# Exchanging the resident operand of a seven-product matmul kernel: blocks in pairs in place of plain blocks

## The chip, the cores and the metric

The kernel runs on one core of a Trainium2 chip. The metric is the device time of one execution in microseconds, taken as the median of several runs. The inputs are fixed random arrays, all fp32.

## The reference

The reference is one layer of an encoder over 2048 tokens of 1024 channels: token mixing, cross-attention into 256 memory tokens, and a feed-forward network, each between two RMS norms and added to the residual stream.

```python
u = rms_norm(h, g_mix_pre); z = u @ w_in              # 1024 -> 2816
ya = swa_with_sinks(...)                              # window attention, 8 heads of 64
yh = hgrn2(...)                                       # gated recurrence, 4 heads of 128
y = concatenate([ya, yh]) @ w_out                     # 1024 -> 1024
h = h + rms_norm(y, g_mix_post)
u = rms_norm(h, g_x_pre); m = rms_norm(mem, g_mem)
y = cross_attention(u, m, wq, wk, wv, wo)             # 4 heads of 256
h = h + rms_norm(y, g_x_post)
u = rms_norm(h, g_ffn_pre)
y = (silu(u @ w_gate) * (u @ w_up)) @ w_down          # 1024 -> 2816 -> 1024
h = h + rms_norm(y, g_ffn_post)
```

## The kernel before

**Precision and products.** TensorE multiplies fp32r operands, so each fp32 operand is split into a rounded part and a rest (`split2`, line 871: ACT or POOL rounds, line 874 or 876, and DVE subtracts, line 877). A product of two such operands is three matmuls per tile of 128 rows (`products`, lines 1004 to 1006). On top of that the large matrix products use the Strassen-Winograd scheme: a block of 256 rows by 1024 columns is cut in two by two, and is made of seven half-size products (`seven`) where the plain way takes eight (`eight`). With four k tiles a product of half size is twelve matmuls, so a seven-product block has 84 and a plain one 96; with three k tiles it is 63 and 72.

**Operands.** Each product has a streamed side S and a resident side T. The S of a block come from two raw tiles (`streamed`, pool tag `raw`), from which DVE forms four sums (`combine`, line 979, tag `sum`) and `made` splits seven S tiles. The T tiles are 128 x 2 x 4 x 512 and serve all blocks of a job. There are seven slots for them. The seven T of a job are three quarters of the operand itself (keys 1, 2, 3) and four sums of quarters (keys 5, 7, 6, 4, `CHAIN`); a plain block needs the fourth quarter, key 8, and none of the sums.

**Jobs.** `jobs` lists what runs after the mixing stage: the output projection, the cross-attention scores with folded weights (`qk_d`), its values (`vo_d`), the feed-forward's first layer for two halves of the tokens (`ffn_u(b)`; here the tokens are the resident side and w_gate and w_up are streamed in turn), and three parts of the down projection (3, 4 and 4 pairs of k tiles). A job is a list of blocks of a kind: `"s"` is seven products, `"p"` is plain. The last block of every job but the last is plain, and so is the first block of the out projection and of the first feed-forward half (`kinds`, nine in all). In such a block the four sum slots are free, so the sums of the next job can be put in them.

**Sums made ahead.** For most jobs the four sums of T are made in an earlier stage and stored in DRAM (`sums` and `combined`, line 921): a tile half is then one load. For the out projection and the first feed-forward half (`None` in the job) they are made on the spot in `resident`: keys 5 and 7 take two loads per half and each sum a DVE operation of 128x1024 (line 903).

**Order.** `phases` writes the order out by hand. For each step it emits the product, then the S splits of the step after next (`upto(need[g + 2])`), then one turn of every generator in `after` (what follows a block: norms, transposes, stores), then the split of a T half that is due, and the loading of the next T half if a slot is free (`half`). T halves lie in row tiles (tag `row`, nine of them, used for results too) until they are split, two steps later. `behind` queues an instruction behind the last marked ones of ACT and DVE. When the program is built, a planner may put instructions of one engine in another order than the source has. In a seven-product block the steps are 1, 5, 6, 3, 7, 2, 4: products 1, 6, 7 and 4 accumulate in one PSUM bank, which ACT copies out after 1 and after 6 (line 1019), 5 and 3 in a second bank, 2 in a third. Six banks are for products and two for transposes.

**Ahead of the jobs** stand the input projection's first half (`in_first`, the same scheme), its second half beside the window attention and the recurrence (`in_proj`, `swa`, `hgrn`), and the folding of the cross-attention weights beside the rest of the recurrence (`fold_cross`). DMAs are issued from SP (lines 75 and 78), except those that add into a tile (line 1350), from POOL. Tokens pass from stage to stage as transposed tensors in DRAM: `y_d`, `h1t_d`, `pt_d`, `u_d`, each `[8, 128, 2048]`, so that a token tile of 128 is read and written in pieces of 512 B, and a block of 256 tokens in pieces of 1 KB.

Of the kernel before, what the change touches and what calls it, by code (L numbers as in the profile page):

```python
# [48 lines left out]
class Layer:  # L49
# [116 lines left out]
    def run(self):  # L166
# [4 lines left out]
        self.y_d = tc.dram_tile([KT, P, T], F32, name="y_d")  # L171
        self.un_d = tc.dram_tile([KT, P, TB], F32, name="un_d")
        self.h1t_d = tc.dram_tile([KT, P, T], F32, name="h1t_d")
        self.pt_d = tc.dram_tile([KT, P, T], F32, name="pt_d")
# [22 lines left out]
    def mix(self):  # L197
        tc, I = self.tc, self.I
        kw = dict(reuse_waits="tile")
        with contextlib.ExitStack() as left:  # L200
# [5 lines left out]
            with (  # L206
                tc.tile_pool(name="t1", bufs=3, **kw) as self.ts,
                tc.tile_pool(name="t2", bufs=3, **kw) as self.tb,
                tc.tile_pool(name="s1", bufs=2, side="right", **kw) as self.st_pool,
                contextlib.ExitStack() as at,  # L210
            ):
                self.banks(at, "ps1", **MOST)
                self.raws = 3
                u = self.in_first()
# [4 lines left out]
            with tc.tile_pool(name="sw", bufs=1, side="right", **kw) as self.sw:  # L219
# [16 lines left out]
            phases = self.phases(self.jobs(), None, lambda: self.io_tile("z"))  # L236
# [10 lines left out]
            with (  # L247
# [6 lines left out]
                self.raws = 4  # L254
# [151 lines left out]
    def in_first(self):  # L406
# [72 lines left out]
        blocks = [("q" if i == 0 else "p" if i < 2 else "s",)  # L479
# [34 lines left out]
    def in_block(self, ca, cb, beside, get, between):  # L514
# [19 lines left out]
        def out(i, j, a, b):  # L534
# [14 lines left out]
            else:  # L549
                self._n += 1  # L550
                t = self.st_pool.tile([P, 512], F32, tag="part", name=f"th_{self._n}", bufs=3)
# [163 lines left out]
    def swa_back(self, n, kinds, S, vs):  # L715
# [25 lines left out]
        self.store(self.y_d[0:4, :, n * P:(n + 1) * P].rearrange("k p t -> p k t"), ys)  # L741
# [84 lines left out]
    def hgrn_last(self, n, kinds, on, sg):  # L826
# [6 lines left out]
        self.store(self.y_d[4:8, :, n * P:(n + 1) * P].rearrange("k p t -> p k t"), sg)  # L833
# [33 lines left out]
    STEPS = {"s": (1, 5, 6, 3, 7, 2, 4), "p": (1, 2, 8, 3), "q": (1, 2, 8, 3)}  # L867
    TAKES = {"s": (1,) * 7, "p": (2, 2, 0, 0), "q": (4, 0, 0, 0)}
# [83 lines left out]
    def streamed(self, load, nk, kind, engine=None, tiled=False):  # L952
# [14 lines left out]
        yield None  # L967
# [8 lines left out]
        def combine(a, b, op):  # L976
            self._n += 1
            t = self.st_pool.tile([P, 4, P], F32, tag="sum", name=f"sum_{self._n}", bufs=3)[:, :nk, :]
# [7 lines left out]
        yield made(a11, "A")  # L986
        s1 = combine(a21, a22, ALU.add)
# [3 lines left out]
        yield made(combine(a12, s2, ALU.subtract), "A")  # L991
        yield made(combine(a11, a21, ALU.subtract), "P")
        yield made(a12, "A")
# [14 lines left out]
    def seven(self, S, T, nk, out, addend):  # L1008
# [6 lines left out]
        def copy(ps, i, j):  # L1015
            self._n += 1
            t = self.st_pool.tile([P, 512], F32, tag="part", name=f"part_{self._n}", bufs=3)
# [6 lines left out]
        for p in self.STEPS["s"]:  # L1024
# [60 lines left out]
    def phases(self, jobs, first, prologue=None):  # L1085

        steps = [(n, i, p) for n, job in enumerate(jobs) for i, b in enumerate(job[2])
                 for p in self.STEPS[b[0]]]  # L1090
        takes = [c for job in jobs for b in job[2] for c in self.TAKES[b[0]]]
        need = list(itertools.accumulate(takes)) + [sum(takes)] * 2
# [79 lines left out]
        blocks = [b for job in jobs for b in job[2]]  # L1172
        streams, ready, made = [], [], [0]

        def stream(at):
            if at < len(blocks):
                streams.append(blocks[at][1](blocks[at][0]))
                next(streams[-1])

        def upto(count):  # L1180
            while made[0] < count:
                s = next(streams[0], None)
                if s is None:
                    streams.pop(0)
                    continue
                ready.append(s)
# [9 lines left out]
        for i in range(2):  # L1196
            upto(need[i])
# [3 lines left out]
        at = 0  # L1201
        self.last = {}
        for _, nk, bl, _, beside in jobs:
            for i, (kind, _, out, follow, addend) in enumerate(bl):
                stream(at + 1)
                after += [f() for f in beside.get(i, ())]
                run = (self.seven(ready, Ready(), nk, out, addend) if kind == "s" else
                       self.eight(ready, Ready(), nk, out, addend, kind == "q"))
                for q in range(len(self.STEPS[kind])):
                    next(run)  # L1210
                    self.mark()
                    upto(need[g + 2])
                    for _ in range(1 if kind == "s" else 2):
# [10 lines left out]
                after.append(follow())  # L1224
                at += 1
# [20 lines left out]
    def jobs(self):  # L1246
# [24 lines left out]
        def sums(name, src, nk, other=None):  # L1271
            dst = self.tc.dram_tile([4, P, nk * 512], F32, name=name)

            def get(which, i, j, k0, n):
                t = (self.extra_tile, other or self.gain_tile)[which]().rearrange("p (k d) -> p k d", d=512)[:, :n]
# [10 lines left out]
        qk_s, vo_s = sums("qk_s", qk, 4, self.row_tile), sums("vo_s", vo, 4)  # L1286
        u_s = sums("u_s", ffn_u(1), 4)
        d_s = [sums(f"d_s{c}", src, nk) for c, (src, _, nk) in enumerate(down)]
        jobs = [(w_out, 4, kinds([self.mixed_block(n) for n in range(0, NT, 2)], 1), None, {2: [qk_s[1]]}),
                (qk, 4, kinds([self.score_block(n) for n in range(0, NT, 2)]), qk_s[0], {1: [vo_s[1]]}),  # L1290
                (vo, 4, kinds([self.value_block(n) for n in range(0, NT, 2)]), vo_s[0], {})]
        for b in range(NB):
            beside = {2: [in_turn(*(d[1] for d in d_s))]} if b else {4: [u_s[1]]}
            jobs.append((ffn_u(b), 4, kinds([blk for f in range(0, NFF, 2) for blk in self.hidden_blocks(b, f)], 1 - b),
                         u_s[0] if b else None, beside))
# [303 lines left out]
```

## Time and profile before

| what | value |
|---|---|
| median of 3 runs | 2636.8 us (2635.38 to 2640.75) |
| the profiled execution | 2634.33 us |
| its span in the trace | 2632.6 us |
| TensorE busy | 2555.3 us (97%), 12265 instructions |
| VectorE busy | 1712.0 us (65%) |
| ScalarE busy | 1261.0 us (48%) |
| granted TensorE clock, mean | 0.992 |

The span is what the trace covers; the execution's own time is 1.7 us longer. Busy shares are means over stages with different limits. In the trace of this kernel the lines 1004 to 1006 are the matmuls of the blocks, 877 and 874 the splits, 979 the sums of S, 1019 the copies of partial products, 1239 the transposes. The out projection's products run from about 795 us, the scores' from about 1000, the values' from about 1165, the feed-forward's from about 1345, the down projection's from about 2200 us.

### The profile page before, as it was taken

The numbers are of one execution on the slowest core, as the hardware profiler recorded it, in microseconds if no ns is written. First come the engines' busy times: TensorE is split into PE (matmuls) and PEld (weight loads), VectorE is DVE, ScalarE is ACT, GpSimd is POOL, SyncE is SP. The second block draws the span as 40 slices with busy tenths as digits, with TensorE's granted clock in tenths as the row PEclk, the third lists the DMA queues.
The fourth block names the chain that finished last, engine by engine and source line by source line (L and its number), as shares of the span: only waits on it lengthen the run. The fifth ranks groups of instructions, "written<-read, shape, count | busy, mean of one in ns | idle before, by whom it ended". The sixth has DMA issues, their size and how long they took to land.

```text
span 2632.6 us, 34672 instructions
## 1 busy us (share of the span) xinstructions
PE 2555.3 (97%) x12265; PEld 2129.9 (81%) x12265; DVE 1712.0 (65%) x2693; ACT 1261.0 (48%) x2620; POOL 465.6 (18%) x651
## 2 busy tenths in 40 slices
PE   7999999999999999999989999999999999999998
PEld 6877888887987777888878888888888888888886
DVE  7675578876556658777666655566666656574656
ACT  5463366655554556565564333344333334453543
POOL 4240344321412323323310000000000000000022
PEclk9999999999999999999999999999999999999999
DMA  5434655444887998776893632253556435576888
GB/s 184 145 130 167 201 153 164 131 155 151 254 292 207 285 284 256 213 243 176 227 285 129 192 111 80 98 192 127 168 198 202 153 117 176 179 216 179 266 209 215
DMA packets 331628, 494.46 MB, mean 188 GB/s; under 512 B 20416, under 2 KB 204736, under 8 KB 331456
## 3 DMA queue, kind: packets, MB, share of 16 engines
q1 hardware_dynamic: 320800, 453.46, 52.1%
q0 software_dynamic: 10656, 38.80, 8.2%
q8 instruction: 96, 1.57, 0.2%
q14 instruction: 76, 0.62, 0.1%
HBM read 333.85 MB, written 158.33 MB: 187 GB/s over the span
## 4 chain that ended last, share of the span: by engine, by line
PE 77%; DMA 11%; DVE 4%; ACT 3%; issue 3%; POOL 2%; SPq 0%; DVEq 0%; POOLq 0%; ACTq 0%
PE psm L1004 21%; PE psm L1005 21%; PE psm L1006 21%; PE psg L163 2%; PE psg L161 2%; PE psg L162 2%; PE pss L1239 1%; DMA z<-in_w_out_dram 1%; DMA h1t_d<-row 1%; DMA row<-in_w_out_dram 1%; DMA u_d<-row 1%; DMA row<-y_d 1%; DMA row<-in_x_dram 1%; DMA row<-u_d 1%; DMA sraw<-in_w_in_dram 1%
## 5 line engine op out<-in xcount | busy, mean ns | idle before, releaser
L1004 PE MATMUL psm<-T,S 128*128 128x512 f32 x2699 | 1049.3, 393 | 17.7 <-ACT part L1019 7.1
L1005 PE MATMUL psm<-T,S 128*128 128x512 f32 x2699 | 1054.6, 391 | 6.4 <-DVE T L877 6.4
L1006 PE MATMUL psm<-T,S 128*128 128x512 f32 x2699 | 1045.9, 391 | 2.1 <-DVE S L877 2.1
L1004 PEld LDWEIGHTS psm<-T,S 128*128 128x128 f32 x2699 | 509.3, 189 | 131.5 <-ACT part L1019 8.7
L1005 PEld LDWEIGHTS psm<-T,S 128*128 128x128 f32 x2699 | 509.2, 189 | 113.0 <-DVE T L877 8.6
L1006 PEld LDWEIGHTS psm<-T,S 128*128 128x128 f32 x2699 | 508.9, 189 | 109.8 <-DVE S L877 4.4
L877 DVE TENSOR_TENSOR S<-sraw,S 128x512 fp32r<-128x512 f32 (+1 forms) x320 | 222.9, 703 | 219.2 <-ACT S L874 199.7
L874 ACT ACTIVATE S<-sum 128x512 fp32r<-128x512 f32 (+1 forms) x310 | 186.1, 618 | 343.0 <-PE psm L1006 245.8
L877 DVE TENSOR_TENSOR S<-sum,S 128x512 fp32r<-128x512 f32 (+1 forms) x368 | 247.6, 683 | 58.4 <-ACT S L874 37.7
L1019 ACT ACTIVATE part<-psm 128x512 f32<-128x512 f32 x270 | 159.8, 596 | 244.1 <-PE psm L1006 225.2
L874 ACT ACTIVATE S<-sraw 128x512 fp32r<-128x512 f32 (+1 forms) x273 | 168.0, 617 | 122.4 <-PE psm L1006 103.5
L1350 POOL DMA_DIRECT2D row<-y_d x28 | 25.9, 926 | 1123.7 <-DVE row L1523 1038.3
L877 DVE TENSOR_TENSOR T<-row,T 128x1024 fp32r<-128x1024 f32 (+1 forms) x122 | 144.2, 1195 | 63.1 <-ACT T L874 62.7
L1321 ACT ACTIVATE junk<-row 128x512 f32<-128x512 f32 x160 | 99.9, 626 | 89.0 <-DVE row L1343 29.7
L161 PE MATMUL psg<-u,whi 128*128 128x512 f32 x352 | 141.1, 401 | 1.1 <-POOL whi L145 1.1
L163 PE MATMUL psg<-u,wlo 128*128 128x512 f32 x352 | 139.6, 397 | 1.5 <-DVE wlo L146 1.5
L162 PE MATMUL psg<-u,whi 128*128 128x512 f32 x352 | 139.5, 396 | 0.0
L874 ACT ACTIVATE T<-row 128x1024 fp32r<-128x1024 f32 x122 | 122.2, 1027 | 31.3 <-DVE row L903 20.4
L876 POOL TENSOR_SCALAR S<-sum 128x512 fp32r<-128x512 f32 x58 | 49.9, 860 | 232.7 <-PE psm L1006 166.0
L146 DVE TENSOR_TENSOR wlo<-raw,whi 128x1024 fp32r<-128x1024 f32 x54 | 68.5, 1269 | 26.0 <-ACT whi L143 18.1
L979 DVE TENSOR_TENSOR sum<-sraw,sraw 128x512 f32<-128x512 f32 (+1 forms) x92 | 63.5, 691 | 30.7 <-DMA sraw<-h1t_d 8.1
L1474 DVE TENSOR_TENSOR row<-psm,part 128x512 f32<-128x512 f32 x63 | 41.7, 687 | 59.1 <-PE psm L1006 58.9
(325 smaller groups left out, 3578.2 us busy)
## 6 DMA issues: line engine op xcount, KB each, us to landing
sraw<-in_w_gate_dram SPq DMA_DIRECT2D x44, 512.0 KB, 3.4
sraw<-in_w_up_dram SPq DMA_DIRECT2D x44, 512.0 KB, 3.4
hid_d<-row SPq DMA_DIRECT2D x44, 512.0 KB, 2.7
h_d<-row SPq DMA_DIRECT2D x32, 512.0 KB, 5.7
y_d<-row SPq DMA_DIRECT2D x32, 512.0 KB, 3.0
sraw<-hid_d SPq DMA_DIRECT2D x32, 512.0 KB, 5.3
row<-h_d POOLq DMA_DIRECT2D x30, 512.0 KB, 6.4
row<-u_d SPq DMA_DIRECT2D x30, 512.0 KB, 6.6
```

Of the source, the lines that this page charges most:

```text
L146: nc.vector.tensor_tensor(lo, raw, f32(hi), ALU.subtract)
L161: nc.tensor.matmul(ps, ah, bh, start=(i == 0), stop=False)
L162: nc.tensor.matmul(ps, ah, bl, start=False, stop=False)
L163: nc.tensor.matmul(ps, al, bh, start=False, stop=(i == n - 1))
L874: self.nc.scalar.activation(hi, raw, AF.Copy)
L877: self.nc.vector.tensor_tensor(lo, raw, f32(hi), ALU.subtract)
L979: nc.vector.tensor_tensor(t, a, b, op)
L1004: nc.tensor.matmul(ps, s[:, 0, k, :], t[:, 0, k, :], start=st, stop=False, **kw)
L1005: nc.tensor.matmul(ps, s[:, 0, k, :], t[:, 1, k, :], start=False, stop=False, **kw)
L1006: nc.tensor.matmul(ps, s[:, 1, k, :], t[:, 0, k, :], start=False, stop=sp, **kw)
L1019: nc.scalar.activation(t, ps, AF.Copy)
L1321: self.nc.scalar.activation(junk, a, AF.Square, scale=float(D) ** -0.5, accum_out=to)
```

## The change

No block of the jobs is plain any more. Instead there is a kind `"d"`: two blocks one after the other in the list run in turn, step by step, so that each T serves two steps in a row. Each job begins with two such blocks and ends with two (the last job only begins with them), and the blocks between are `"s"`. The steps of `"s"` and `"d"` become 1, 2, 5, 6, 7, 3, 4, with the S tiles made in that order; the input projection keeps the old order under the name `"o"`, with its plain blocks. The sums of w_out are made beside the second half of the window attention (`w_sums`, four turns after each of its pairs of tiles but the first), those of the first feed-forward half in `value_block` for the token tiles 4 to 7, which reads the tiles 0 to 3 of `u_d` back and stores the four sums in `u_s0`. `y_d`, `h1t_d` and `pt_d` are laid out by token tile, `[16, 128, 8, 128]`. In the jobs stage there are six raw tiles (four before), four `part` tiles (three) and five `sum` tiles (three).

```diff
-        self.y_d = tc.dram_tile([KT, P, T], F32, name="y_d")
+        self.y_d = tc.dram_tile([NT, P, KT, P], F32, name="y_d")
...
+                jobs = self.jobs()
+                sums = self.w_sums()
                 swa = self.swa(range(NPB, NT), "sth")
-                for _ in swa:
+                for i, _ in enumerate(swa):
                     next(cols)
+                    if i:
+                        self.mark()
+                        for _ in range(4):
+                            next(sums, None)
                 for _ in cols:
                     pass
+                for _ in sums:
+                    pass
...
-                self.raws = 4
+                self.raws, self.parts, self.sums = 6, 4, 5
...
-    STEPS = {"s": (1, 5, 6, 3, 7, 2, 4), "p": (1, 2, 8, 3), "q": (1, 2, 8, 3)}
-    TAKES = {"s": (1,) * 7, "p": (2, 2, 0, 0), "q": (4, 0, 0, 0)}
+    STEPS = {"o": (1, 5, 6, 3, 7, 2, 4), "s": (1, 2, 5, 6, 7, 3, 4), "d": (1, 2, 5, 6, 7, 3, 4), "p": (1, 2, 8, 3), "q": (1, 2, 8, 3)}
+    TAKES = {"o": (1,) * 7, "s": (1,) * 7, "d": (1,) * 7, "p": (2, 2, 0, 0), "q": (4, 0, 0, 0)}
...
-        steps = [(n, i, p) for n, job in enumerate(jobs) for i, b in enumerate(job[2])
-                 for p in self.STEPS[b[0]]]
...
+        for n, job in enumerate(jobs):
+            i = 0
+            while i < len(job[2]):
+                members = (i, i + 1) if job[2][i][0] == "d" else (i,)
+                groups.append((n, members))
+                i += len(members)
+        steps, takes = [], []
+        for n, members in groups:
+            kind = jobs[n][2][members[0]][0]
+            for p, c in zip(self.STEPS[kind], self.TAKES[kind]):
+                for i in members:
+                    steps.append((n, i, p))
+                    takes.append(c)
...
-                for q in range(len(self.STEPS[kind])):
-                    next(run)
+            for q in range(len(self.STEPS[kind])):
+                for i in members:
+                    next(runs[i])
                     self.mark()
-                    upto(need[g + 2])
+                    upto(g + 2)
...
-        def kinds(blocks, n=0):
-            return [("p" if i < n or i == len(blocks) - 1 else "s",) + b for i, b in enumerate(blocks)]
+        def kinds(blocks, first="dd", last="dd"):
+            middle = "s" * (len(blocks) - len(first) - len(last))
+            return [(k,) + b for k, b in zip(first + middle + last, blocks)]
...
         return lambda kind: self.streamed(lambda t, j: self.load(
-            t, src[4 * j:4 * j + 4, :, n * P:(n + 2) * P].rearrange("k p t -> p k t")), 4, kind)
+            t, src[n:n + 2, :, 4 * j:4 * j + 4].rearrange("i p k t -> p i (k t)")), 4, kind, tiled=True)
...
-                self.store_transposed(self.u_d, n + i, self.transposed(u[i], u[i]))
+                tv = self.transposed(u[i], u[i])
+                self.store_transposed(self.u_d, n + i, tv)
+                if 4 <= n < 8:
+                    o.append(self.row_tile().rearrange("p (k t) -> p k t", k=KT))
+                    self.load(o[i], self.u_d[:, :, (n + i - 4) * P:(n + i - 3) * P].rearrange("k p t -> p k t"))
+                yield
+            for i in range(len(o)):
+                tv = u[i].rearrange("p (k t) -> p k t", k=KT)
+                s = self.row_tile().rearrange("p (k t) -> p k t", k=KT)
+                with self.behind():
+                    nc.vector.tensor_tensor(s[:, 0:4], tv[:, 0:4], o[i][:, 0:4], ALU.subtract)
+                    nc.vector.tensor_tensor(s[:, 4:8], tv[:, 4:8], tv[:, 0:4], ALU.subtract)
+                yield
+                with self.behind():
+                    nc.vector.tensor_tensor(o[i][:, 0:4], o[i][:, 0:4], s[:, 4:8], ALU.add)
+                    nc.vector.tensor_tensor(o[i][:, 4:8], o[i][:, 4:8], o[i][:, 0:4], ALU.subtract)
+                at = slice((n + i - 4) * P, (n + i - 3) * P)
+                for c, t in enumerate((s[:, 0:4], s[:, 4:8], o[i][:, 0:4], o[i][:, 4:8])):
+                    self.store(self.u_s[c][:, :, at], t)
                 yield
```

More of the change, by code (lines that the diff above doesn't have):

```diff
@@ L1170, in __getitem__, with upto @@
                 return T[key]
-        blocks = [b for job in jobs for b in job[2]]
-        streams, ready, made = [], [], [0]
+        streams, ready, made = {}, {}, [0]
         def stream(at):
[L1176 to L1186, printed above, removed]
+            if at < len(groups):
+                n, members = groups[at]
+                for i in members:
+                    b = jobs[n][2][i]
+                    streams[n, i] = b[1](b[0])
+                    ready[n, i] = []
+                for _ in range(2):
+                    for i in members:
+                        next(streams[n, i])
+        def upto(g):
+            while made[0] < min(g + 1, len(steps)):
+                n, i, _ = steps[made[0]]
+                for _ in range(takes[made[0]]):
+                    ready[n, i].append(next(streams[n, i]))
                 made[0] += 1
```

92 lines of the change are left out of this document (52 added, 40 removed).

## The prediction

> **What bounds the kernel now.** I read the page first: busy shares, then the costliest groups.
>
> ```profile
> span 2632.6 us, 34672 instructions
> ...
> PE 2555.3 (97%) x12265; PEld 2129.9 (81%) x12265; DVE 1712.0 (65%) x2693; ACT 1261.0 (48%) x2620; POOL 465.6 (18%) x651
> ...
> L1004 PE MATMUL psm<-T,S 128*128 128x512 f32 x2699 | 1049.3, 393 | 17.7 <-ACT part L1019 7.1
> ```
>
> TensorE is busy 97% of the span, so only two things can shorten the kernel: fewer matmuls, or fewer gaps between them. The 393 ns of a matmul is not its price, because matmuls overlap. The price is the distance between starts, which the timeline of PE in an undisturbed stretch shows:
>
> ```profile
> 1001.03 0.39 PE L1004 MATMUL psm<-T,S 128*128 128x512 f32 x1
> ...
> 1003.75 0.39 PE L1004 MATMUL psm<-T,S 128*128 128x512 f32 x1
> ```
>
> Between these two rows stand twelve starts (lines 1004, 1005, 1006 four times, one product of four k tiles): 2.72 us for twelve, 0.2267 us each. One step of a seven-product block is 2.72 us, such a block 84 x 0.2267 = 19.0 us.
>
> Next, busy time by stretch, chosen by where lines first appear: out projection, scores, values, the two feed-forward halves, down projection, and the second half of the window attention ahead of them.
>
> ```profile
> 460.00:645.00 185.00, 183.35 (x973) 154.33 (x973) 145.74 (x357) 112.17 (x301) 46.97 (x76) 1.00 0.44 136
> ...
> 795.00:1000.00 205.00, 187.34 (x842) 150.51 (x841) 126.63 (x151) 106.65 (x231) 64.47 (x92) 0.96 0.92 267
> 1000.00:1165.00 165.00, 164.44 (x787) 136.28 (x786) 125.44 (x227) 93.07 (x224) 44.70 (x58) 1.00 0.75 230
> 1165.00:1365.00 200.00, 193.87 (x914) 160.05 (x912) 137.16 (x166) 117.33 (x251) 56.52 (x87) 1.00 0.79 227
> 1365.00:1780.00 415.00, 413.00 (x1810) 340.44 (x1811) 252.71 (x364) 162.58 (x275) 0.00 (x0) 0.99 0.41 140
> 1780.00:2200.00 420.00, 420.00 (x1855) 347.77 (x1854) 261.98 (x382) 159.64 (x275) 0.00 (x0) 1.00 0.49 165
> ```
>
> The columns are PE, PEld, DVE, ACT and POOL, then granted clock, DMA share and GB/s. From 1365 to 2200 PE has no gap worth the name. The out projection has: at the score stage's rate (164.44 us for 787 records of the same mix, 0.209 us each) its 842 records are 176 us, and it took 205. It loses 29 us, at 92% DMA share. The second place is the change from values to feed-forward:
>
> ```profile
> 1040.00:1060.00 20.00, 20.00 (x99) 16.67 (x98) 17.36 (x35) 10.50 (x28) 5.71 (x6) 1.00 0.67 205
> 1320.00:1365.00 45.00, 39.87 (x191) 32.77 (x189) 29.79 (x32) 26.52 (x52) 8.47 (x15) 0.99 0.96 284
> 1365.00:1390.00 25.00, 23.00 (x89) 17.51 (x90) 22.06 (x25) 16.33 (x26) 0.00 (x0) 0.81 0.64 219
> 1740.00:1800.00 60.00, 60.00 (x266) 49.71 (x265) 43.48 (x54) 33.38 (x48) 0.00 (x0) 1.00 0.56 195
> 1900.00:1938.00 38.00, 38.00 (x169) 31.47 (x168) 24.59 (x37) 13.52 (x25) 0.00 (x0) 1.00 0.62 209
> ```
>
> 191 x 0.209 + 89 x 0.2267 = 60 us of work in 70 us: 10 us lost, and the clock falls to 0.81 there. The change at 1740 to 1800, covered by a plain block, loses nothing. What PE waits for (us in total, times, longest), first from 795 to 900, then from 900 to 1020, then from 1330 to 1385:
>
> ```profile
> PE psm L1005 <- DVE T L877: 5.3, 2, 3.6
> ```
> ```profile
> PE pss L1239 <- ACT row L1240: 5.2, 1, 5.2
> PE pss L1239 <- DMA row<-in_x_dram: 2.6, 3, 1.1
> ```
> ```profile
> PE psm L1004 <- ACT T L874: 3.5, 2, 3.2
> PE pss L1239 <- DVE row L1452: 2.2, 1, 2.2
> ```
>
> So the T operands are late where their sums are made on the spot (two loads and a subtraction for one tile half), and transposes stand in PE's queue behind late rows.
>
> **The change, part by part.** Plain blocks: nine go (out projection two, scores one, values one, feed-forward two and one, the first two parts of the down projection one each). Eight drop from 96 matmuls to 84, the one with three k tiles from 72 to 63: 8 x 12 + 9 = 105 matmuls, 105 x 0.2267 = **-23.8 us**. PE is the bound where they stand, so this counts in full unless a wait takes the place.
>
> What the plain block covered is the exchange of the T tiles, and the pair must cover it now. A tile's last use in the outgoing pair is step 2q+1 of fourteen, its first use in the incoming pair step 14+2q: twelve steps lie between, 33 us, for two loads, two ACT copies and two DVE subtractions. Prices:
>
> ```profile
> L877 DVE TENSOR_TENSOR S<-sum,S 128x512 fp32r<-128x512 f32 x340 | 232.2, 694 | 49.0 <-ACT S L874 28.3 <-POOL S L876 18.7
> L877 DVE TENSOR_TENSOR T<-row,T 128x1024 fp32r<-128x1024 f32 x114 | 139.0, 1231 | 59.4 <-ACT T L874 59.0
> L979 DVE TENSOR_TENSOR sum<-sraw,sraw 128x512 f32<-128x512 f32 x85 | 59.6, 702 | 29.5 <-DMA sraw<-h1t_d 8.1 <-DMA sraw<-in_w_in_dram 7.0 <-PE psh L323 3.7
> L1474 DVE TENSOR_TENSOR row<-psm,part 128x512 f32<-128x512 f32 x63 | 41.7, 687 | 59.1 <-PE psm L1006 58.9
> ```
>
> Each block that turns from plain to seven costs DVE three more S splits (0.694), four sums (0.702) and three additions (0.687), 6.9 us beside PE. DVE at a change of the feed-forward: two pairs are 4 x 19.0 = 76 us; its own work is twice 24.59 (the row 1900 to 1938 is two blocks), the T splits 14 x 1.231 = 17.2, together 66, or 87%. In the row 1040 to 1060 DVE is busy 87% and PE has no gap; in 1365 to 1390 it is busy 88% and PE loses time. So the cover is just enough. Bounds for the seven changes are nothing and 3 us each (the longest waits for T above are 3.2 and 3.6), 20 us; I take a little under 1 us each, **+6**, nearer to the rows 1040 and 1740. A pair also holds four raw tiles, six PSUM banks (all six of their kind) and four row tiles of nine; I count their waits in this term: where two pairs meet, eight raw tiles are wanted and six are there, so the last loads wait on SP, and behind them T loads and stores.
>
> Out projection: its four sums come ready from DRAM, so a half is one load, and the first pair uses each T for two steps. The 5.3 us for T go. What stays is DMA:
>
> ```profile
> DMA packets 35973, 54.72 MB, mean 267 GB/s; under 512 B 1820, under 2 KB 21889, under 8 KB 35961
> ...
> row<-in_w_out_dram SPq DMA_DIRECT2D x20, 256.0 KB, 8.5
> ...
> row<-in_w_out_dram SPq DMA_DIRECT2D x4, 512.0 KB, 6.8
> ```
>
> These weight loads are 7.3 MB; three tiles remain (the prologue takes four), 3.1 MB, so 50.5 MB are left. The rows by token tile make pieces of 512 B and 1 KB into 2 and 4 KB. A full DMA share is worth 267/0.92 = 290 GB/s here and 140/0.41 = 341 GB/s in the feed-forward with its long pieces: 174 or 148 us. PE needs 176 - 5.4 = 171. So the stage can fall to about 174, or, if only the plain blocks go, to 200. The waits for the late rows and the accumulated x (5.2 and 2.6) remain as mechanisms. I take the middle, 185: beyond the plain blocks **-15**, bounds 0 and -29.
>
> Values to feed-forward: the first half's sums come ready, so the T wait of 3.5 goes, the transposes' wait less surely: of 10 us I take **-6**, bounds 0 and -10.
>
> The moved sums. The eight combinations of w_out go beside the window attention, with twelve loads and eight stores of at most 512 KB on SP's queue: 10 MB, at a DMA share of 0.44 hidden. On DVE they are eight operations of 128x1024; the T split of that shape is 1.231, so 10 us on 145.7 of 185 us. They stand behind marked instructions, and if a load is late DVE waits with everything behind it, the splits that PE needs among them; the stores hold SP until the sums are there. Bounds nothing and 10 us (each one seen in full by PE); I take **+3**, since DVE has 21% spare. The sums of u for four token tiles: sixteen DVE operations of about 0.7, 11 us on 137 of 200, four loads and sixteen stores of 256 KB on SP, 6 MB against the 4 MB that the ready sums save. Bounds 0 and 11; **+1**, because the stage keeps 25% of DVE.
>
> Order of steps. In the single blocks step 7 now follows step 6 on the same bank, and between them ACT must copy it; the old order had step 3 there. There are 62 single blocks (4, 4, 4, 18, 18, 4, 4, 6). What such a wait costs:
>
> ```profile
> 1015.50 0.40 PE L1006 MATMUL psm<-T,S 128*128 128x512 f32 x1
> 1015.77 0.57 ACT L1019 ACTIVATE part<-psm 128x512 f32<-128x512 f32 x1
> ...
> 1016.40 0.19 PEld L1004 LDWEIGHTS psm<-T,S 128*128 128x128 f32 x1 [0.29 <-ACT part L1019]
> ```
> ```profile
> 1004.20 0.41 PEld L1004 LDWEIGHTS psm<-T,S 128*128 128x128 f32 x2
> ```
>
> The weight load that waited for the copy starts 0.90 us after the last matmul instead of 0.23: 0.7 us, times 62 is 43. But PE's queue is not the source order: two L1004 stand in a row in the last fence, where the source gives 1004, 1005, 1006, so the planner already moves matmuls of another product ahead when one isn't ready. Step 3 is on another bank, and its S is made two steps ahead; four of its matmuls fill the hole. Bounds 0 and 43; I take **+3**, near the stretch 1365 to 2200, where such moves leave no gap.
>
> The Trainium skill, page "PSUM — Partial Sum Buffer", sections "PSUM bank collisions raise a hardware error" and "Engine vs sequencer instructions", says that a bank must be guarded between its writer and its reader, and that matmuls start in program order, so a blocked one holds all behind it. By that rule alone every single block would pay the wait; the row at 1016.40 agrees that the wait exists, and the sum would end on the slower side (third rival).
>
> The sum, against the profiled execution of 2634.3 us (its span 2632.6): -23.8 - 15 - 6 + 6 + 3 + 1 + 3 = -31.8, 2602.5. The median of the runs, 2636.8, lies 2.5 above that execution, so the forecast is **2605**.
>
> **The rivals.** (1) More goes: all 29 and 10 us vanish and the costs hide, 2636.8 - 23.8 - 39 = 2574; with half of the costs (13 us) about 2580. For it speaks that T was the largest wait; against it the 92% DMA share.
>
> (2) The gain is given back at the changes: three us at each of seven for T, banks or rows, and the DMA-bound stage keeps 8 us more: 2605 + 14 + 8 = 2627. For it: 88% DVE in 1365 to 1390 with PE waiting. Against: 1040 to 1060.
>
> (3) Slower: PE really stands between steps 6 and 7, because step 3 isn't ready where the planner looks. 62 x 0.7 = 43 in place of my 3: 2605 + 40 = 2645. It passes the kernel before where a block loses (2637 - 2602)/62, 0.56 us. For it the price row; against it the interleaved row.
>
> (4) The change doesn't do what it says: the planner runs the blocks of a pair one after the other. Then a tile has five steps, 14 us, and each of the seven changes loses some 10 us, as values to feed-forward did: 2605 + 70 - 6 = about 2670. Nothing speaks for it but that the order is re-planned.
>
> **How the numbers follow.** Chances: forecast (2592 to 2617) 0.50, more goes 0.18, given back 0.18, slower by step 7 0.11, not in turn 0.03. The range leaves out half of the first rival and most of the last two: 2580 to 2645. About 0.2% (5 us) can be told from no change by measurement. Faster: 0.50 + 0.18 + most of the second rival, 0.81; within 0.2% 0.05; slower 0.14.
>
> **What would show it.** Matmuls on lines 1004 to 1006 fall by 105 (8097 records before). Out projection: about 185 us instead of 205, no wait on T at its start, fewer packets under 2 KB. Changes at scores, values and feed-forward: PE waits on T under 3 us each; if DVE there is at 90% with waits on T or banks, rival 2. Waits of L1004 for ACT part L1019 in each single block would be rival 3. The window attention should be at most 10 us longer. Wrong would be the whole account if PE's gaps in the feed-forward, now none, exceed 20 us.

## The result, and the profile after

The changed kernel takes 2612.7 us in the median of four runs (2605.43 to 2614.87), the kernel before 2637.05 beside it: a ratio of 0.9901 (0.9879 to 0.9923), 24 us less. Run again beside other kernels, it took 2608.8 us against 2639.9, 0.9881 (0.9863 to 0.99). The profiled execution of the changed kernel is 2605.4 us, the lowest of its runs, so small differences are read from the repeat too.

The page of the changed kernel; the line numbers moved by 8 to 34 (the matmuls of the blocks are now lines 1018 to 1020, the splits 882 and 885, the sums of S 987, the copies of partial products 1033, the transposes 1270 with their copies on 1271, the additions that make the rows of the out projection and of the values 1377, and the mean squares 1355):

```profile
span 2603.6 us, 34511 instructions
...
PE 2526.8 (97%) x12160; PEld 2112.8 (81%) x12160; DVE 1744.2 (67%) x2773; ACT 1262.3 (48%) x2641; POOL 473.4 (18%) x651
...
DMA packets 286350, 497.88 MB, mean 191 GB/s; under 512 B 20576, under 2 KB 143456, under 8 KB 286176
...
L1018 PE MATMUL psm<-T,S 128*128 128x512 f32 x2664 | 1034.9, 392 | 24.6 <-ACT S L882 13.5
L1019 PE MATMUL psm<-T,S 128*128 128x512 f32 x2664 | 1041.1, 391 | 0.0
```

The second of the three matmul lines on the page of the kernel before, for comparison:

```profile
L1005 PE MATMUL psm<-T,S 128*128 128x512 f32 x2699 | 1054.6, 391 | 6.4 <-DVE T L877 6.4
```

PE has 12265 - 12160 = 105 instructions fewer, and its busy time falls by 28.5 us. The share of the span is still 97%. The idle time ahead of the first matmul line no longer has the copies of partial products as its largest cause, but the S tiles; and ahead of the second line the 6.4 us of waiting for T are gone.

Busy time by stretch, the kernel before (columns as in the prediction; the counts behind x are the records of a stretch, and a stretch that loses time holds fewer of them; the stretches are fixed in time, so where a stage ends late the next stretch holds the rest of its work):

```profile
1000.00:1280.00 280.00, 278.45 (x1321) 230.27 (x1320) 210.45 (x335) 160.01 (x371) 81.34 (x113) 1.00 0.71 212
1280.00:1420.00 140.00, 132.86 (x602) 108.40 (x601) 91.67 (x108) 78.51 (x150) 19.88 (x34) 0.96 0.77 237
1420.00:2140.00 720.00, 720.00 (x3178) 596.20 (x3177) 439.75 (x643) 267.95 (x460) 0.00 (x0) 1.00 0.44 150
2140.00:2590.00 450.00, 448.31 (x1974) 369.90 (x1974) 265.29 (x386) 201.07 (x354) 39.37 (x53) 1.00 0.68 200
260.00:645.00 385.00, 379.07 (x2069) 322.10 (x2068) 291.28 (x706) 222.03 (x628) 130.11 (x192) 1.00 0.52 157
```

and the changed kernel:

```profile
260.00:645.00 385.00, 375.84 (x2055) 319.56 (x2056) 294.46 (x707) 218.48 (x622) 129.14 (x192) 1.00 0.59 183
...
795.00:1000.00 205.00, 190.27 (x863) 156.10 (x864) 138.47 (x175) 109.52 (x237) 65.19 (x94) 0.97 0.86 274
1000.00:1280.00 280.00, 276.23 (x1322) 228.90 (x1321) 218.00 (x352) 163.09 (x385) 83.07 (x115) 1.00 0.72 224
1280.00:1420.00 140.00, 131.74 (x600) 108.32 (x599) 102.26 (x134) 78.55 (x153) 23.32 (x32) 0.98 0.73 226
1420.00:2140.00 720.00, 720.00 (x3178) 595.92 (x3177) 439.36 (x648) 273.42 (x468) 0.00 (x0) 1.00 0.44 147
2140.00:2590.00 450.00, 448.10 (x1975) 369.88 (x1974) 285.49 (x419) 202.67 (x371) 47.42 (x63) 1.00 0.69 200
```

Two things are to be seen. From 1000 us on, PE works at the same rate as before, with all plain blocks gone: the same number of matmuls lies in each stretch, and in 1420 to 2140 there is no gap. So the shorter stream is paid in full. But the two places where the prediction wanted more have hardly changed. The out projection's stretch holds 863 records where it held 842 (the row is in the prediction): 21 x 0.209 = 4.4 us, not 15. At the change from values to feed-forward PE is idle 140 - 131.7 = 8.3 us, before 7.1.

Why not, the waits of PE show. Changed kernel, 780 to 880, and then 1270 to 1370:

```profile
PE psm L1018 <- ACT S L882: 6.9, 1, 6.9
```

```profile
PE psm L1018 <- ACT S L882: 6.6, 2, 4.5
```

The waits for T are gone from both places, as foreseen, and a wait for S stands where each was (in a second profile of the same kernel, below called the repeat, 7.0 and 7.7 us). Later in the out projection, from 880 to 1010, the largest wait is that for the added residual x, ahead of the transposes:

```profile
PE pss L1270 <- DMA row<-in_x_dram: 4.6, 2, 2.5
```

The timeline at the start of the out projection (start, duration, then engine or queue, in brackets the idle time before and what ended it):

```profile
783.75 11.32 SPq L78 DMA_DIRECT2D vo_d<-x  x5
...
795.17 1.25 SPq L75 DMA_DIRECT2D sraw<-y_d  x2
...
801.17 0.63 ACT L882 ACTIVATE S<-sraw 128x512 fp32r<-128x512 f32 x1 [5.46 <-DMA sraw<-y_d]
...
801.85 0.79 PE L1018 MATMUL psm<-T,S 128*128 128x512 f32 x1 [6.89 <-ACT S L882]
```

SP stands 11.3 us at stores of the folded weights, which wait for the copies by ACT (15.1 us in seven waits from 770 to 800). The first loads of `y_d` are queued behind them, at 795.2 us where the kernel before issued its first at 760.2, and PE starts 6.9 us late. At the second place ACT stands. Its waits from 1270 to 1350:

```profile
ACT junk L1355 <- DMA row<-h_d: 14.1, 5, 5.2
ACT junk L1355 <- DVE row L1377: 9.7, 3, 6.2
```

The mean squares of the value rows wait for the added residual (a transfer that adds `h_d` into the row), and behind them in ACT's queue stand the roundings of S that PE needs. From 1330 to 1352 one of these waits, of 4.4 us, meets one of PE's:

```profile
ACT junk L1355 <- DMA row<-h_d: 5.5, 2, 4.4
```

```profile
PE psm L1018 <- ACT S L882: 4.5, 1, 4.5
```

ACT's wait for the added residual is not new, but it has grown: in the kernel before it is 6.0 us, three times, from 1300 to 1385.

### The profile page after: what moved, and what is told of

Its sections match the earlier page's. It is cut to its first block, busy times and chain, and to the rows that moved or that the text cites. A ratio compares the mean times of both kernels' runs of the same rounds, so it can differ in the third digit from the quotient of the medians.

```text
span 2603.6 us, 34511 instructions
## 1 busy us (share of the span) xinstructions
PE 2526.8 (97%) x12160; PEld 2112.8 (81%) x12160; DVE 1744.2 (67%) x2773; ACT 1262.3 (48%) x2641; POOL 473.4 (18%) x651
## 2 busy tenths in 40 slices
DMA packets 286350, 497.88 MB, mean 191 GB/s; under 512 B 20576, under 2 KB 143456, under 8 KB 286176
## 4 chain that ended last, share of the span: by engine, by line
PE 80%; DMA 8%; DVE 4%; issue 3%; POOL 2%; ACT 2%; SPq 0%; DVEq 0%; POOLq 0%; ACTq 0%
PE psm L1018 22%; PE psm L1020 22%; PE psm L1019 22%; PE psg L161 2%; PE psg L163 2%; PE psg L162 2%; DMA row<-in_x_dram 1%; PE pss L1270 1%; DMA row<-h_d 1%; ACT junk L1355 1%; DMA x<-in_w_out_dram 1%; DVE S L885 1%; DMA h_d<-row 1%; DMA pair<-in_x_dram 1%; DMA kk<-z_d 1%
## 5 line engine op out<-in xcount | busy, mean ns | idle before, releaser
L1018 PE MATMUL psm<-T,S 128*128 128x512 f32 x2664 | 1034.9, 392 | 24.6 <-ACT S L882 13.5
L1019 PE MATMUL psm<-T,S 128*128 128x512 f32 x2664 | 1041.1, 391 | 0.0
L1020 PE MATMUL psm<-T,S 128*128 128x512 f32 x2664 | 1036.1, 391 | 3.8 <-DVE S L885 3.8
L1018 PEld LDWEIGHTS psm<-T,S 128*128 128x128 f32 x2664 | 502.2, 189 | 132.7 <-ACT S L882 15.3
L1020 PEld LDWEIGHTS psm<-T,S 128*128 128x128 f32 x2664 | 501.9, 188 | 111.0 <-DVE S L885 6.9
L1019 PEld LDWEIGHTS psm<-T,S 128*128 128x128 f32 x2664 | 502.3, 189 | 103.0
L882 ACT ACTIVATE S<-sum 128x512 fp32r<-128x512 f32 (+1 forms) x338 | 208.1, 619 | 341.4 <-PE psm L1020 333.1
L885 DVE TENSOR_TENSOR S<-sraw,S 128x512 fp32r<-128x512 f32 (+1 forms) x311 | 214.2, 696 | 223.4 <-ACT S L882 213.4
L885 DVE TENSOR_TENSOR S<-sum,S 128x512 fp32r<-128x512 f32 (+1 forms) x404 | 276.8, 689 | 81.6 <-ACT S L882 63.7
L1033 ACT ACTIVATE part<-psm 128x512 f32<-128x512 f32 x297 | 175.1, 592 | 178.0 <-PE psm L1020 172.8
L885 DVE TENSOR_TENSOR T<-row,T 128x1024 fp32r<-128x1024 f32 x104 | 123.1, 1191 | 30.5 <-ACT T L882 30.2
L882 ACT ACTIVATE T<-row 128x1024 fp32r<-128x1024 f32 x104 | 105.7, 1027 | 20.7 <-DMA row<-in_w_down_dram 10.3
L1536 DVE TENSOR_TENSOR part<-psm,part 128x512 f32<-128x512 f32 x66 | 45.4, 688 | 65.3 <-PE psm L1020 65.2
L146 DVE TENSOR_TENSOR wlo<-raw,whi 128x1024 fp32r<-128x1024 f32 x54 | 68.7, 1271 | 29.1 <-ACT whi L143 22.4
```

Source lines behind the costliest of these rows:

```text
L146: nc.vector.tensor_tensor(lo, raw, f32(hi), ALU.subtract)
L882: self.nc.scalar.activation(hi, raw, AF.Copy)
L885: self.nc.vector.tensor_tensor(lo, raw, f32(hi), ALU.subtract)
L1018: nc.tensor.matmul(ps, s[:, 0, k, :], t[:, 0, k, :], start=st, stop=False, **kw)
L1019: nc.tensor.matmul(ps, s[:, 0, k, :], t[:, 1, k, :], start=False, stop=False, **kw)
L1020: nc.tensor.matmul(ps, s[:, 1, k, :], t[:, 0, k, :], start=False, stop=sp, **kw)
```

## The experiments

The theory (A): the pairs cover the exchange of T, so the 105 matmuls are paid in full; the two further gains failed because the wait for T was replaced by a wait for S, behind SP at the first place and behind ACT at the second. The rivals: the gain comes from the other parts (ready sums, buffers, layout) and not from the pairs; the new order of steps costs time; the losses lie in DMA traffic and not in what stands in a queue. Where an expectation names letters, A is this theory and the others are its rivals there. All differences below are against the repeat of the changed kernel (2608.8 us) unless said.

**The changed kernel again.** No edit.

> The changed kernel as it is, once more, as the measure for the others. Theory A (the gain is the 105 matmuls, 23.8 us; what PE loses at the exchanges only changed its cause): about 2612, 24 us under the kernel before. Theory B (sums made ahead and rows by token tile brought the gain, the pairs cost about what the plain blocks cost): the same time.

2608.8 us (2603.32 to 2613.29). Its stretches, for comparison with those of the experiments:

```profile
260.00:645.00 385.00, 379.30 (x2053) 322.15 (x2052) 294.64 (x708) 218.03 (x621) 130.08 (x192) 0.99 0.59 183
645.00:795.00 150.00, 141.85 (x1045) 133.50 (x1044) 80.28 (x106) 84.88 (x188) 39.39 (x42) 0.98 0.76 251
795.00:1000.00 205.00, 189.56 (x856) 155.42 (x855) 135.75 (x170) 109.31 (x235) 61.68 (x91) 0.97 0.85 270
1000.00:1280.00 280.00, 276.43 (x1326) 229.13 (x1325) 219.92 (x354) 162.21 (x383) 83.04 (x116) 1.00 0.72 225
1280.00:1420.00 140.00, 131.48 (x595) 107.96 (x594) 101.12 (x132) 78.91 (x155) 24.11 (x33) 0.96 0.74 225
2140.00:2590.00 450.00, 448.06 (x1975) 370.01 (x1974) 284.07 (x420) 204.81 (x374) 44.46 (x61) 1.00 0.69 199
```

**The old order of steps in the single blocks.**

```diff
-            middle = "s" * (len(blocks) - len(first) - len(last))
+            middle = "o" * (len(blocks) - len(first) - len(last))
```

> The single blocks go back to the step order 1, 5, 6, 3, 7, 2, 4; pairs keep the new one. A: step 7 right after step 6 costs nothing, because the planner fills the hole: within 3 us of the changed kernel. Rival (PE stands for the copy between 6 and 7 in each of 62 blocks, 0.3 to 0.7 us): 20 to 40 us faster than the changed kernel.

2624.7 us, 0.9943 (0.9928 to 0.9959) of before: 16 us slower, outside A's expectation and the opposite of the rival. The time is lost in the last part of the down projection (2440 to 2590 holds 592 records for 651 in the repeat, 2140 to 2440 one fewer). The stretch of the down projection and its waits of PE (2180 to 2620) are

```profile
2140.00:2590.00 450.00, 439.97 (x1915) 359.99 (x1913) 272.61 (x403) 198.62 (x360) 42.55 (x57) 0.99 0.67 196
```

```profile
PE psm L1018 <- DVE row L1576: 6.0, 5, 2.0
PE psm L1018 <- ACT S L882: 3.3, 3, 2.2
```

60 records fewer than in the repeat are 13.6 us. Line 1576 is the addition that frees a block's bank; in the repeat PE waits 1.6 us for it there. So beside pairs the new order helps, at this one place; why the old one loses there is not shown.

**No pairs, seven products everywhere.**

```diff
-        def kinds(blocks, first="dd", last="dd"):
+        def kinds(blocks, first="", last=""):
```

> All blocks of the jobs are single seven-product blocks, no pairs and no plain blocks. A: the same 105 matmuls are gone, but a T tile has five steps (14 us) for its exchange and 14 splits of 1.05 us on ACT and 1.23 us on DVE fall into 19 us: 3 to 10 us lost at each of seven changes, 2633 to 2680. B, or if the pair isn't needed as a cover: within 5 us of the changed kernel.

2665.5 us, 1.0094 (1.0076 to 1.0112): 57 us slower with the same matmuls, inside A's expectation. Scores and values, and the change to the feed-forward, show it:

```profile
1000.00:1280.00 280.00, 265.16 (x1227) 215.77 (x1226) 207.06 (x331) 155.88 (x357) 71.56 (x103) 0.98 0.65 200
1280.00:1420.00 140.00, 122.41 (x534) 98.50 (x533) 98.37 (x127) 76.30 (x158) 32.92 (x45) 0.91 0.87 261
```

99 and 61 records fewer than in the repeat, some 20 and 14 us in two stretches alone. Spread over seven changes it is 57/7 = 8 us for an uncovered exchange, as a mean: the stretches show that the changes lose unequally.

**Plain blocks back, the rest of the change kept.**

```diff
-        def kinds(blocks, first="dd", last="dd"):
+        def kinds(blocks, first="", last="p"):
...
-kinds([self.mixed_block(n) for n in range(0, NT, 2)])
+kinds([self.mixed_block(n) for n in range(0, NT, 2)], "p")
```

(and so for the first feed-forward half; the last job has none at its end).

> The nine plain blocks come back in their old places and the pairs go; sums made ahead, rows by token tile, step order and tile counts stay as changed. A: 24 us slower than the changed kernel, so about 2636, the time of the kernel before. B: the other parts carry the gain, so it stays within 8 us of the changed kernel.

2651.2 us, 1.0047 (1.0031 to 1.0062). Both expectations missed: 42 us slower than the changed kernel, and 11 to 14 slower than the kernel before, which has as many matmuls. With the rest of the change in place the pairs are thus worth more than their 24 us, and what else was changed costs something without them. One suspect was the order of steps:

**Plain blocks back and the old order.** The edit of the plain blocks and that of the old order together.

> The nine plain blocks back, no pairs, and the single blocks in the old step order as well; sums made ahead, rows by token tile and tile counts as changed. If the other parts of the change gain nothing by themselves: 2630 to 2640, as the kernel before. If they carry part of the gain: 2620 or less. The plain blocks with the new order took 2651; if the new order alone is what cost there, this one is 10 us or more faster than that.

2653.2 us, 1.0058 (1.0045 to 1.007), outside all that was expected. The order is not the cause. About half of the loss of 14 us against the kernel before is the late start of the out projection again: its first product starts at 801.1 us, in the kernel before at 794.4, and PE's largest wait from 760 to 1010 is the one ahead of it,

```profile
PE psm L1018 <- POOL S L884: 7.0, 1, 7.0
```

(with the new order 7.1 us, the product at 805.7). The rest is spread over the stages (in 1000 to 1280 there are 1286 records for 1321, in 2140 to 2590 1959 for 1974) and stays open.

**The old layout of the three tensors.** `y_d`, `h1t_d` and `pt_d` as `[KT, P, T]`, read and written in pieces of 512 B and 1 KB.

> The three token tensors go back to the layout by channel tile (pieces of 512 B and 1 KB); the rest as changed. A: DMA is busy 0.72 to 0.86 of the time in the out projection, scores and values, so the longer pieces are worth a little there: 0 to 6 us slower than the changed kernel. B: they carry a good part of the gain, 10 us or more slower.

2609.3 us, 0.988 (0.9864 to 0.9896): no difference, though the packets are those of the small pieces,

```profile
DMA packets 339598, 497.88 MB, mean 191 GB/s; under 512 B 20576, under 2 KB 217184, under 8 KB 339424
```

53,248 more than with rows by token tile. The prediction had let the longer pieces carry part of the out projection's gain; they carry none.

**Sums of the first feed-forward half on the spot.**

```diff
-                         u_s[0] if b else self.u_s.rearrange("c p k t -> c p (k t)"), beside))
+                         u_s[0] if b else None, beside))
...
-                if 4 <= n < 8:
+                if False:
```

> The first feed-forward half makes its four sums on the spot again and the value blocks make none; the rest as changed. A: PE's loss at the change from values to feed-forward (12 us in both kernels) hangs on the accumulate of h1, not on the sums: within 4 us of the changed kernel. B: without the sums ahead the change loses 5 to 15 us more.

2616.2 us, 0.9911 (0.9898 to 0.9924): 7.4 slower, outside A's expectation and inside B's. The place is the change itself:

```profile
1280.00:1420.00 140.00, 127.83 (x559) 103.43 (x558) 101.87 (x127) 74.63 (x146) 26.08 (x32) 0.94 0.71 211
```

36 records fewer than in the repeat, 36 x 0.2267 = 8.2 us. The ready sums did not better the kernel before at this place, but the pair can't do without them.

**Four raw tiles.**

```diff
-                self.raws, self.parts, self.sums = 6, 4, 5
+                self.raws, self.parts, self.sums = 4, 4, 5
```

> Four raw tiles in place of six; the rest as changed. The first products of the out projection wait 6.9 us for loads of y_d that are issued only when the stage ahead gives its memory free. If the two more raw tiles are what moved these loads past that point, that wait goes (7 us less there), and each meeting of two pairs may lose 1 to 3 us, 13 such places at most: between 5 us faster and 15 slower. If the loads wait for the queue of SP alone, the wait of 6.9 us stays.

2636.2 us, 0.999 (0.9979 to 1.0001): the whole gain is gone, 27 us, well outside the 15 that were expected at most. PE's wait of 6.9 us ahead of the out projection goes too (the first load of `y_d` is issued at 769.0 us, though the first product starts at 803.1, hardly before the 804.9 of the repeat), but the later changes pay:

```profile
1280.00:1420.00 140.00, 127.16 (x573) 103.27 (x572) 100.11 (x131) 77.68 (x155) 25.71 (x35) 0.96 0.79 235
...
2140.00:2590.00 450.00, 440.40 (x1924) 362.51 (x1923) 269.08 (x404) 199.34 (x357) 37.51 (x50) 0.99 0.66 194
```

22 and 51 records fewer. Two blocks in turn hold four raw tiles, so the next S can't be loaded ahead: from 2440 to 2620 DVE waits 33.0 us for loads of raw tiles (four times) where the sums of S are formed, and in the repeat not at all.

**Raw tiles in a pool of their own, opened first.** Six tiles, at another place in memory, before the pool of the other working tiles.

```diff
-            t = self.ts.tile([P, 4, 256], F32, tag="raw", ...
+            t = self.tr.tile([P, 4, 256], F32, tag="raw", ...
```

> The changed kernel with its six raw tiles in a memory pool of their own, opened first, so that they lie where the stage ahead gives memory free early and their first loads stand ahead of the last eight stores of the folded weights on SP's queue. If the wait of 7 us before the first products of the out projection is this queueing: 5 to 8 us faster than the changed kernel, about 2603. Rival (PE waits there for something else next, for instance the T tiles): within 2 us.

2606.7 us (2602.28 to 2609.47), 0.9877 (0.9864 to 0.989): 2 us faster than the changed kernel, within the noise, where more was expected. PE's wait at the start (790 to 830) shrinks from 6.9 to

```profile
PE psm L1020 <- ACT S L884: 1.3, 1, 1.3
```

(here each line has moved by 2), so the cause of that wait is shown: with tiles in this place the first `y_d` loads are issued at 766.2 us, ahead of the stores. But the wait was not what set the start. The stretches before and after tell where the rest went:

```profile
645.00:795.00 150.00, 138.38 (x1023) 129.48 (x1023) 79.17 (x105) 82.53 (x185) 39.27 (x42) 0.98 0.80 265
795.00:1000.00 205.00, 195.58 (x888) 160.17 (x887) 140.72 (x175) 112.97 (x242) 63.60 (x92) 0.98 0.83 262
```

22 records fewer than in the repeat in the stage ahead, where PE is busy 3.5 us less and DMA more. The 32 records more in the second stretch are not a gain of the out projection: about 20 of them are the rest of the folding, which ends at about 802 us where it ended at 798, so that the first product starts at 803.6, in the repeat at 804.9. The loads come earlier and the folding of the weights becomes longer; that they slow it is likely from the DMA share, but not shown.

**Mean squares later.** In the blocks of the out projection and of the values, two turns later and behind the marked instructions.

```diff
+            yield
+            yield
...
-                self.mean_squares(y[i], i, s2)
+                with self.behind():
+                    self.mean_squares(y[i], i, s2)
```

> In the blocks of the out projection and of the values, the mean squares of a row come two turns later and behind the marked instructions. A: ACT stands up to 4.4 us for the accumulate of h1 or x, and the S splits queued behind it make PE wait (4.5 us before the feed-forward, 10 us in the out projection in several pieces): 5 to 12 us faster than the changed kernel. Rival (the loss is DMA time itself, or DVE's): within 3 us, or slower because rows are held longer.

2622.4 us, 0.9941 (0.9926 to 0.9957): 13.6 slower, where faster was expected. ACT waits for the added rows no longer, but PE waits (1150 to 1350) for copies of partial products:

```profile
PE psm L1018 <- ACT part L1033: 7.8, 4, 3.1
```

in the changed kernel these copies cost PE 0.4 us in the same window. So the late work moved to another place in the queue; that it is this work that holds up the copies there was not traced.

**Three `part` and three `sum` tiles.** As before the change, with six raw tiles.

> The changed kernel with three part tiles and three sum tiles as before the change (six raw tiles stay). If two interleaved blocks need the added tiles as they need the raw ones (four raw tiles cost 27 us): 10 us or more slower than the changed kernel. If raw tiles alone are scarce: within 4 us.

2623.4 us, 0.9946 (0.9932 to 0.996): 15 slower, as expected if the pairs need the added tiles. Scores and values hold 1280 records for 1326:

```profile
1000.00:1280.00 280.00, 270.79 (x1280) 224.22 (x1279) 212.84 (x343) 161.44 (x381) 79.17 (x115) 0.98 0.71 220
```

**The residuals added into an unused tile**, on the kernel with three `part` and `sum` tiles (a tile `aside` found room there).

```diff
-                self.add(y[i], self.I["x"], n + i)
+                self.add(self.aside, self.I["x"], n + i)
...
-                self.add(y[i], self.h1_d, n + i)
+                self.add(self.aside, self.h1_d, n + i)
```

> As the kernel with three part and three sum tiles, but the accumulates of x and h1 in the out projection's and the values' blocks go to a tile that nothing reads: the residual is left out of these rows, the DMA traffic stays, and no engine waits for its landing. If the waits of ACT and of the transposes for these accumulates are what PE still loses in the out projection (14 to 17 us beside the start) and before the feed-forward (12 us): 12 to 25 us faster than that kernel. Rival (DMA time or DVE sets these losses): within 4 us of it.

2631.7 us, 0.9978 (0.9968 to 0.9988): 8 slower than the last one, where faster was expected. As nothing orders them any more, the planner put the transfers of x in the first stage:

```profile
aside<-in_x_dram POOLq DMA_DIRECT2D x16, 512.0 KB, 5.6
```

There the first stretch has 996 records for 1112 of the last experiment, and the out projection starts 28 us later (829.6 us for 801.3); but the change from values to feed-forward loses nothing any more:

```profile
0.00:260.00 260.00, 216.77 (x996) 178.72 (x997) 164.18 (x205) 117.54 (x196) 89.89 (x123) 0.95 0.62 178
...
1280.00:1420.00 140.00, 138.60 (x653) 114.87 (x652) 114.50 (x148) 87.48 (x178) 29.20 (x36) 1.00 0.74 240
```

PE is idle 1.4 us there instead of 8.5. From the first product of the out projection to the last product of the kernel it takes 1791.6 us instead of 1806.2: behind the late start it is 14.6 us faster, inside the 12 to 25 that were expected. That speaks for the added residual as the cause of that loss. Whether its wait or its traffic does it isn't told apart, as both left the place.

## Why the prediction was right

The forecast was 2605, the kernel takes 2612.7 (2608.8 in the repeat): the likeliest case. The largest term and the cover by the pairs were right in their mechanism. Of the rest, gains of 21 us and costs of 13 were forecast, 8 us net, and both were too high: the stretches from 0 to 2590 us hold 12140 records before, 12156 after and 12138 in the repeat, so beside the removed matmuls the change brought some 3.5 us (16 x 0.2267) or nothing. That the errors of these terms nearly cancel is luck.

- **The removed matmuls, -23.8: right.** 105 instructions are gone, and the stretches from 1000 us show the same rate as before, so they are paid in full. The argument behind it, that PE is the bound where the plain blocks stood, held because the pairs cover the exchange: without them the same 105 matmuls fewer took 57 us more.
- **Out projection, -15: mis-sized; measured some -4** (21 records, 14 in the repeat). The step that failed is "The 5.3 us for T go. What stays is DMA": in the place of T came S, 6.9 us late behind SP's stores, and the wait for the added x grew from 2.6 to 4.6 us. The lower of the two bounds from DMA share rested on longer pieces, which give nothing; what PE loses here are waits for single late operands. With the wait for S mended PE starts only 1.3 us earlier than in the repeat, because the folding ahead then ends later.
- **Values to feed-forward, -6: failed; measured 0.** "The T wait of 3.5 goes" is true; PE then waits 6.6 us for S, behind ACT's mean squares. Two experiments that moved or removed what those wait for changed the loss: with the mean squares later it was no smaller and the kernel slower, without the added residual it was gone.
- **The changes, +6: mis-sized; about +2.** In 1000 to 1280 PE is idle 3.8 us instead of 1.6, in the feed-forward never, in 2140 to 2590 1.9 instead of 1.7. This is the cover of the pairs at work (the changes from out projection to scores and from values to feed-forward lie outside these stretches and are in the two terms above). Its conditions, which the prediction only counted as holding tiles, were the larger prices: six raw tiles 27 us, the added `part` and `sum` tiles 15.
- **Sums of w_out, +3: right.** In 260 to 645 there are 14 records fewer (16 in the repeat), 3 us at 0.209.
- **Sums of u, +1:** not seen by itself; undoing both the making and the use costs 7.
- **Order of steps, +3: mis-sized; the wait that it prices was not seen.** There is no gap in 1420 to 2140, where more than half of the single blocks stand. The old order is no better with plain blocks (2653.2 for 2651.2 us) and 16 us slower beside pairs, where the term had let the new one cost something.

Of the rivals, **slower by step 7** is refuted: from 780 us to the end PE waits 0.4 us in all for copies of partial products (1.8 in the repeat), and the rival wanted 43. PE's order in the built program, in the first feed-forward half (matmuls in a row, PSUM tile, T by its key; the listing begins in one single block and ends in the next, whose step 1 is the line of ten):

```
12 bank A  T 1
12 bank B  T 2
12 bank C  T 5
12 bank A  T 6
12 bank C  T 3
10 bank D  T 1
12 bank A  T 7
 2 bank D  T 1
```

The planner puts all of step 3 and ten matmuls of the next block between 6 and 7: 22 x 0.2267 = 5 us, against a hole of 0.7. The Trainium skill, page "PSUM — Partial Sum Buffer", section "Engine vs sequencer instructions", says that matmuls start in program order; the 720 us without a gap don't contradict it, since the program's order is the planned one and not that of the source. **Not in turn** is refuted by the same program: at the pair with which this job begins, twelve matmuls of one block and twelve of the other follow on T 1, the same on T 2 and on T 5, and on T 6 they go 2, 2, 10 and 10. **Given back at the changes** did not happen: from 780 us on PE's waits for T fell from 9.9 us to none, and those for banks and rows hardly grew; the two waits that appeared were for S. **More goes** did not happen because of these two.

Open remain about half of the 14 us that the rest of the change costs with plain blocks, the loss by the old order beside pairs, and the part of wait and traffic in the added residual.

## What to carry to other kernels

Where one engine was busy 97% and stayed so, work taken from it was paid in full, at the distance between starts and not at an instruction's duration; but a gain hoped for from a wait that goes is only worth the distance to the next late operand, so list all operands of the instruction that waits and where each stands in its queue. Two blocks in turn on one operand are a cover for exchanging it that costs no extra matmuls, and are paid for in buffers: without the two added raw tiles the same order gained nothing. Adding buffers, or placing them elsewhere, also moves loads in their queue (the first load of `y_d` stood at 795.2 us with six raw tiles, at 769.0 with four, at 766.2 in a pool of its own), so the first transfers of a stage are to be looked at again after it. And a fixed stretch that holds more work isn't a faster stage: find where the stage starts.

## What was not expected of the hardware

Moving the same 497.88 MB in 286,350 packets instead of 339,598 changed nothing (2608.8 and 2609.3 us), in a kernel whose DMA share is 0.85 in the out projection. And a store queue held up one stage from the one before: five stores took SP 11.3 us, and the loads behind them made PE, the bound, wait 6.9. Yet with the loads ahead of the stores PE started only 1.3 us earlier.
